# A decoder layer's first and last 40 microseconds, and the row stride of one operand

## The chip, the cores and the metric

The kernel runs on one core of a Trainium2 chip. The metric is the device time of one execution in microseconds. The kernel is one program, launched once, that computes the whole layer step in float32 (matrix products with operands split into two fp32r parts, see below).

## The reference, cut to what matters

One layer of a hybrid decoder is applied to 256 prompt tokens (one sequence) and to 64 sample tokens (8 sequences of 8, with past states). Both share all weights.

```python
D_MODEL = 2048; D_FF = 5504; LN_EPS = 1e-5; ALPHA = 2 ** 0.25

def layer(x, st, p):
    u = x @ w_in                                  # 2048 -> 6680
    q, k, v, o_pre, i_pre, f_pre, z, xbc, dt_pre = split_columns(u, SPLIT_SIZES)
    h_m, ... = mlstm_mixer(q, k, v, o_pre, i_pre, f_pre, ...)   # i_pre, f_pre: gates, 8 columns
    h_s, ... = ssd_mixer(z, xbc, dt_pre, ...)                   # dt_pre: 16 columns
    mix = concatenate([h_m, h_s]) @ w_out
    x = layer_norm(ALPHA * x + mix, ln1_g, ln1_b)
    f, fconv = conv_ffn(x, w_up, f_conv_w, f_conv_b, w_down, fconv0)   # 2048 -> 11008 -> 2048
    x = layer_norm(ALPHA * x + f, ln2_g, ln2_b)
    return x, new_states

def layer_norm(x, g, b):
    mu = mean(x); var = mean((x - mu) ** 2)
    return (x - mu) * rsqrt(var + LN_EPS) * g + b
```

## The kernel before, in words

All activations are kept transposed: 128 features on the partitions, 320 tokens (`NT` = 256 prompt + 64 sample) along the free dimension, 16 such blocks for the 2048 features. A product with a weight matrix is made of units of 128 output features. A unit is 16 blocks deep, and for each block there are three matmuls of 320 columns: high part of the weight by high part of the activation, high by low, low by high. Four blocks of a unit, 12 matmuls, are called a chunk here; `run_groups` works on two units in turn (four in the first group), chunk by chunk. For each chunk, `Stream.split_to` makes the high part on ScalarE (line 74) and the low part on VectorE (line 75), up to four chunks ahead of their use (`HB` = 5 buffers), from raw weights that SP's queue loads (line 61) into four buffers of 512 KB, plus four borrowed ones at the start.

Everything that is not such a product is written as background tasks, Python generators. The planner `Tasks` has a clock of its own: every matmul issued adds its estimated nanoseconds, and a task that yields a number sleeps for so many of them. After each chunk `run_groups` calls `tasks.pump`, which lets the tasks that are due issue their instructions. So the program order of every engine is fixed by hand and by this clock when the program is written; on the chip each engine works through its queue in that order.

The places that the change touches:

- The beginning. Nine fp32 matmuls of `ones` run on TensorE while the first loads arrive (`warm`). `x_load` brings x_prompt in four column chunks, `xs_load` brings x_sample into `xs_in`, whose lower 64 partitions hold the features below 1024 and the upper 64 those above. `x_transpose` turns a chunk's four blocks on TensorE (line 238), copies them to `XH` on ScalarE (line 416) and makes the remainder `XL` on VectorE (line 418). Block k < 8 also turns a piece of `xs_in`, which gives the sample columns of block k and of block k + 8. `start_x` and `each_x` place the first four blocks among the first chunk's matmuls, and the later ones ahead of the fourth unit's chunks.
- `keep_x`. For each of the four chunks of x it adds `XH` and `XL` on GpSimd, multiplies by the gate columns `gw` of `w_in` (matmuls with 32 output rows) and stores x to DRAM (`xT`) through SP. `gw` is loaded on SP behind the first eight raw weight tiles (lines 466 and 467), in pieces of 32 and 64 bytes. Ahead of its first chunk the task sleeps for 8000.
- The rows of the first norm. `dd` (the difference from the mean), and `DH` and `DL` (its high and low parts, with gain) are tiles of 16 rows of `NX` = 322 values: 320 tokens, and two further columns for the gain and the bias of the norm, which the first of three groups of up projections multiplies along (322 columns; the other two groups 320). The tile size is shared with the buffers `r01`, `r2`, `g` of the end.
- The end. `down_task` finishes a block of the output, turns it back to tokens on the partitions, takes `bn_stats` of it, and multiplies it by the norm's gain (`times_g`). After block 15, `bn_aggr` over 16 blocks' statistics, the reciprocal root (a square root on ScalarE and Newton steps on VectorE), three rows of factors, turned by TensorE into `nbr`, and a last loop over four column chunks: a matmul with the bias rows, a VectorE operation for the two prompt tiles (line 1676), and for the sample tile a ScalarE scale and copy and a GpSimd addition (lines 1671 to 1674). All stores go through SP.

Of the kernel before, what the change touches and what calls it, by code (L numbers as in the profile page):

```python
# [7 lines left out]
F32R = mybir.dt.float32r  # L8
# [5 lines left out]
NT = 320  # L14
# [156 lines left out]
def _hybrid_step(ctx, tc, I, O):  # L171
# [11 lines left out]
    def f32(ap):  # L183
        return ap.bitcast(F32)
# [199 lines left out]
    box = {}  # L384
    G.memset(ones, 1.0)
    warm = bank()
    for _ in range(9):
        mm(warm[:, 0:128], ones, ones, True, True)

    def x_load(c):  # L390
# [9 lines left out]
    def x_transpose(c, kks=range(4)):  # L400
        t = box["x", c]
        if kks[-1] == 3:
            flags.add(("xt", c))
            del box["x", c]
        for kk in kks:
            k = 4 * c + kk
            ps = bank()
            for i in range(2):
                transpose(ps[:, 128 * i:128 * i + 128], t[:, i, 128 * kk:128 * kk + 128])
            parts = [(k, 0, 256)]  # L410
            if k < 8:
                transpose(ps[:, 256:384], xs_in[:, 128 * k:128 * k + 128])
                parts = [(k, 0, NT), (k + 8, NT, 384)]
            parts = [(kx, slice(256 if a else 0, 256 if b == 256 else NT), ps[:, a:b]) for kx, a, b in parts]
            for kx, o, src in parts:
                A.activation(XH(kx)[:, o], src, AF.Copy)
            for kx, o, src in parts:
                V.tensor_tensor(XL(kx)[:, o], src, f32(XH(kx))[:, o], ALU.subtract)  # L418

    def keep_x():  # L420

        pg = bank()
        for c in range(4):
            yield from wait(("xt", c))
            yield 1000 if c else 8000
            ts = []
            for k in (4 * c, 4 * c + 2):
                t = mt("T4", [128, 2, NT])
                G.tensor_tensor(t, f32(XH(k, 2)), f32(XL(k, 2)), ALU.add)
                ts.append(t)  # L430
            yield 4000
            for kk in range(4):
                mm(pg[32 * kk:32 * kk + 32, 0:NT], gw[:, 4 * c + kk, :], ts[kk // 2][:, kk % 2, :], c == 0, c == 3)
            tasks.clk -= 3 * 541
            for k, t in zip((4 * c, 4 * c + 2), ts):
                dma(xT[:, k:k + 2, :], t)
        yield from gate_task(pg)


    xs_in = mt("T10", [128, 1024])  # L440
    xs_src = I["x_sample"].rearrange("b t f -> (b t) f")

    def xs_load(eng, a, b):
        for e in range(2):
            eng.dma_start(xs_in[64 * e:64 * e + 64, a:b], xs_src[:, 1024 * e + a:1024 * e + b])

    x_load(0)
    xs_load(nc.scalar, 0, 256)
    own = [mt("T4", [128, 1024]) for _ in range(4)]
    st.load(1, own[0:1])  # L450
    dma(box["x", 0][:, :, 256:512], I["x_prompt"][0, :, 256:512].rearrange("(i p) f -> p i f", p=128))
    xs_load(nc.sync, 256, 512)
    st.load(2, own[1:2])
    x_load(1)
    st.load(3, own[2:3])
    xs_load(nc.sync, 512, 1024)
    st.load(4, own[3:4])
    x_load(2)
    st.load(6)
# [846 lines left out]
    def start_x(u, s):  # L1306
        if u == s == 0:
            x_transpose(0, [0])
        if u == 3 and s < 3:
            x_transpose(s + 1)  # L1310

    def each_x(u, s, kk):
        if u == s == 0 and kk < 3:
            x_transpose(0, [kk + 1])


    MH, ML = Halves("MH"), Halves("ML")
# [33 lines left out]


    fp = ctx.enter_context(tc.tile_pool(name="fp", bufs=1))
    NX = NT + 2
    fr = tile_of(fp, {"big": (3, 16 * NX), "c": (12, 346), "rx": (2, 4 * NT), "rows": (2, 2304), "dg": (2, 384)})

    def fsm(shape, dt=F32):
        return fp.tile(shape, dt, name=nm("fsm"))
# [33 lines left out]
        rx[c] = t  # L1392

    load_rx(0)
    dd = fr("big", [128, 16, NX])
    DH, DL = fr("big", [128, 16, NX], F32R), fr("big", [128, 16, NX], F32R)
    s1, s2, kbc = fr("c", [128, NT]), fr("c", [128, NT]), fr("c", [128, NT])

    def out_task(m, ps):
# [153 lines left out]
    def down_task(j, m, ps):  # L1553
# [56 lines left out]
    for j in range(3):  # L1610
# [26 lines left out]

    mv, var, nb2, rs, u = fsm([128, 3, 2]), fsm([128, 3]), fsm([128, 3]), fsm([128, 3]), fsm([128, 3])  # L1640
    nbc, nbr = fsm([128, 3, 5], F32R), fr("dg", [5, 384], F32R)
    G.memset(f32(nbc), 1.0)
    for i in range(3):
        V.bn_aggr(mv[:, i, :], lnst[:, i, :, :])
    A.activation(fin["sd"], mv[:, :, 1], AF.Sqrt, bias=fin["eps"][:, 0:1])
# [7 lines left out]
    V.scalar_tensor_tensor(nb2, mv[:, :, 0], -1.0, rs, ALU.mult, ALU.mult)  # L1653
    V.tensor_copy(nbc[:, :, 0:2], bcl(nb2, 2))
    V.tensor_tensor(nbc[:, :, 2], nb2, f32(nbc[:, :, 0]), ALU.subtract)
    ps = bank()
    for i in range(3):
        transpose(ps[0:5, 128 * i:128 * i + 128], f32(nbc[:, i, :]))
    for i in range(3):
        t = slice(128 * i, 128 * i + 128)  # L1660
        V.tensor_copy(nbr[:, t], ps[0:5, t])
    times_g(15, fin["pt"])
    ys = O["y_sample"].rearrange("b t f -> (b t) f")
    for c in range(4):
        s = slice(512 * c, 512 * c + 512)
        for i in range(3):
            t = fin["r2"][:, s] if i == 2 else fin["r01"][:, i, s]
            w = bank()
            mm(w, nbr[:, 128 * i:128 * i + 128], fin["rows"][:, s], True, True)
            if i == 2:  # L1670
                A.activation(t, t, AF.Copy, scale=rs[64:128, i:i + 1])
                w2 = fr("rx", [128, 512])[64:128]
                A.activation(w2, w[64:128, :], AF.Copy)
                G.tensor_tensor(t, t, w2, ALU.add)  # L1674
            else:
                V.scalar_tensor_tensor(t, t, rs[:, i:i + 1], w, ALU.mult, ALU.add)
# [4 lines left out]
    dma(*late)  # L1681


# [62 lines left out]
```

## Time and profile before

| | |
|---|---|
| median of 3 runs | 1546.82 us (1544.77 to 1548.61) |
| the profiled execution | 1550.87 us, span of its instructions 1549.0 us |
| TensorE matmul / weight load busy | 98% / 96% of the span |
| VectorE, ScalarE, GpSimd busy | 63%, 50%, 20% |
| mean granted TensorE clock | 0.988 |
| moved by DMA | 254.39 MB, 164 GB/s over the span |

Times in the views are microseconds from the first instruction. A timeline row gives start, duration, engine, line, operation, what it writes and reads, the shape, how many instructions it merges, and in brackets how long the engine was idle before it and what ended that. A row of windows gives the window, its length, the busy time and the number of instructions of PE (TensorE matmuls), PEld (its weight loads), DVE (VectorE), ACT (ScalarE) and POOL (GpSimd), then the granted clock as a share of full speed, the DMA share and GB/s. An fp32 matmul appears as two records, so nine of them are 18.

### The profile page before, as it was taken

To read this page: it belongs to the slowest core of one execution; us is meant where nothing else is said; L and a number is where in the kernel's file an instruction comes from. 1 tells how busy PE (TensorE), PEld (TensorE's weight loads), DVE (VectorE), ACT (ScalarE), POOL (GpSimd) and SP (SyncE) were. 2 spreads that over 40 slices of the span, in tenths; PEclk is the share of its full clock that TensorE was granted. 3 is DMA by queue.
4 is the path that set the end of the run, shared out by engine and by line. 5 is a ranking of instruction groups with operands and counts; after the bars stand their busy time and mean duration, and the time that the engine had idled before them with its cause. 6 is when DMAs were issued, how large, how long until landed. Compare 5 with 4: busy or idle time off the path is not lost.

```text
span 1549.0 us, 28113 instructions
## 1 busy us (share of the span) xinstructions
PE 1521.4 (98%) x10518; PEld 1488.8 (96%) x10518; DVE 980.7 (63%) x1959; ACT 773.4 (50%) x1540; POOL 306.1 (20%) x651
## 2 busy tenths in 40 slices
PE   8999999999999999999999999999999999999996
PEld 7999999998999999999999999999999999999995
DVE  4676557666687587687777445566544555656765
ACT  3655434444545454566665345555433555555332
POOL 5213331134411142233330000000000000002201
PEclk8999999999999999999999999999999999999997
DMA  9556677577665554455544454554454555455542
GB/s 252 161 150 163 183 208 225 160 211 226 209 204 174 193 180 138 126 165 149 150 150 140 154 147 146 163 150 138 149 157 146 148 151 163 141 149 170 159 145 77
DMA packets 268900, 254.39 MB, mean 164 GB/s; under 512 B 18513, under 2 KB 263265, under 8 KB 268636
## 3 DMA queue, kind: packets, MB, share of 16 engines
q1 hardware_dynamic: 263612, 248.49, 53.8%
q0 software_dynamic: 4848, 3.91, 1.0%
q8 instruction: 82, 1.34, 0.4%
q14 instruction: 54, 0.44, 0.1%
q10 hardware_dynamic: 304, 0.20, 0.0%
HBM read 231.56 MB, written 20.43 MB: 163 GB/s over the span
## 4 chain that ended last, share of the span: by engine, by line
PE 93%; DVE 2%; DMA 2%; POOL 1%; ACT 1%; issue 1%; SPq 1%; POOLq 0%; DVEq 0%; ACTq 0%
PE bk L232 90%; PE bk L238 2%; DMA T<-w_in 1%; DVE lo L75 1%; DMA rx<-xT 0%; SPq L61 0%; ACT hi L74 0%; POOL big L1674 0%; SPq L466 0%; ACT MH L1320 0%; POOL T L193 0%; POOL T L968 0%; POOL T L811 0%; DVE HL L1531 0%; POOL T L981 0%
## 5 line engine op out<-in xcount | busy, mean ns | idle before, releaser
L75 DVE TENSOR_TENSOR lo<-raw,hi 128x512 fp32r<-128x512 f32 (+2 forms) x800 | 558.0, 708 | 393.5 <-ACT hi L74 390.6
L74 ACT ACTIVATE hi<-raw 128x512 fp32r<-128x512 f32 (+2 forms) x800 | 486.3, 616 | 454.3 <-PE bk L232 429.5
L232 PE MATMUL bk<-big,hi 128*128 128x320 f32 (+1 forms) x2752 | 609.5, 310 | 0.0
L232 PEld LDWEIGHTS bk<-big,hi 128*128 128x128 f32 x2752 | 462.1, 188 | 0.0
L232 PE MATMUL bk<-big,lo 128*128 128x320 f32 (+1 forms) x1376 | 426.6, 310 | 0.4 <-DVE lo L75 0.4
L232 PE MATMUL bk<-XH,hi 128*128 128x320 f32 x832 | 269.0, 323 | 0.8 <-ACT hi L74 0.8
L232 PEld LDWEIGHTS bk<-big,lo 128*128 128x128 f32 x1376 | 259.3, 188 | 0.7 <-DVE lo L75 0.7
L232 PE MATMUL bk<-XL,hi 128*128 128x320 f32 x832 | 258.9, 311 | 0.0
L232 PE MATMUL bk<-XH,lo 128*128 128x320 f32 x832 | 258.8, 311 | 0.0
L232 PE MATMUL bk<-HH,hi 128*128 128x320 f32 x688 | 214.2, 311 | 0.0
L232 PE MATMUL bk<-HH,lo 128*128 128x320 f32 x688 | 212.6, 309 | 0.0
L232 PE MATMUL bk<-HL,hi 128*128 128x320 f32 x688 | 212.5, 309 | 0.0
L232 PEld LDWEIGHTS bk<-XH,hi 128*128 128x128 f32 x832 | 158.1, 190 | 12.0 <-issue 7.9
L232 PEld LDWEIGHTS bk<-XL,hi 128*128 128x128 f32 x832 | 158.1, 190 | 0.9 <-DVE XL L418 0.4
L232 PEld LDWEIGHTS bk<-XH,lo 128*128 128x128 f32 x832 | 157.7, 190 | 0.2 <-DVE lo L75 0.2
L193 POOL TENSOR_SCALAR fst<-c 128x18 f32<-128x18 f32 x86 | 22.5, 269 | 566.9 <-ACT c L1508 566.7
L1515 DVE SCALAR_TENSOR_TENSOR c<-c,fcol,c 128x336 f32<-128x336 f32 x172 | 97.3, 567 | 58.4 <-ACT c L1513 55.3
L232 PEld LDWEIGHTS bk<-HL,hi 128*128 128x128 f32 x688 | 129.2, 188 | 0.0
L232 PEld LDWEIGHTS bk<-HH,hi 128*128 128x128 f32 x688 | 129.2, 188 | 0.0
L232 PEld LDWEIGHTS bk<-HH,lo 128*128 128x128 f32 x688 | 129.1, 188 | 0.0
L232 PE MATMUL bk<-MH,lo 128*128 128x320 f32 x256 | 80.1, 313 | 2.4 <-DVE lo L75 2.4
L232 PE MATMUL bk<-MH,hi 128*128 128x320 f32 x256 | 80.3, 314 | 0.3 <-ACT hi L74 0.3
(330 smaller groups left out, 1470.3 us busy)
## 6 DMA issues: line engine op xcount, KB each, us to landing
raw<-ffn_w_up SPq DMA_DIRECT2D x172, 512.0 KB, 3.9
raw<-w_in SPq DMA_DIRECT2D x100, 512.0 KB, 4.2
raw<-ffn_w_down SPq DMA_DIRECT2D x71, 512.0 KB, 3.5
raw<-w_out SPq DMA_DIRECT2D x32, 512.0 KB, 5.1
T<-state_mlstm_C SPq DMA_DIRECT2D x32, 256.0 KB, 5.5
s_C<-T SPq DMA_DIRECT2D x32, 256.0 KB, 4.0
T<-state_ssm SPq DMA_DIRECT2D x8, 512.0 KB, 6.9
s_ssm<-T SPq DMA_DIRECT2D x8, 512.0 KB, 6.7
```

Source lines behind the costliest of these rows:

```text
L74: nc.scalar.activation(h, src, AF.Copy)
L75: nc.vector.tensor_tensor(l, src, h.bitcast(F32), ALU.subtract)
L193: G.tensor_scalar(out, in_, 1.0, 0.0, ALU.mult, ALU.add)
L232: nc.tensor.matmul(out, lhsT=lhsT, rhs=rhs, start=start, stop=stop)
L238: nc.tensor.transpose(out, in_, ident[b:b + p, b:b + p])
L1515: V.scalar_tensor_tensor(c[:, 0:336], xp[:, j:j + 336], fcol[:, j, i:i + 1], c[:, 0:336], ALU.mult, ALU.add)
```

## The change

- Start: 13 warm matmuls instead of 9, and four more between the second block's transposes and the first real matmul. `xs_in` holds even blocks' features on the lower and odd blocks' on the upper partitions, so each even block's sample transpose gives the sample columns of itself and of the next block; x_sample's loads are cut into 512-byte runs, and the second of them stands behind one weight load instead of ahead of it. The first split of weights is issued ahead of the second block; blocks 3 and 4 of the first chunk are turned together ahead of the second block's matmuls. `keep_x` sleeps for 11500 instead of 8000.
- Rows: `dd`, `DH`, `DL` get rows of `NP` = 336 values (1344 bytes) instead of 322 (1288 bytes).
- End: the statistics of blocks 0 to 14 are aggregated after block 14 and put beside block 15's, so that the last aggregation reads three groups of three values for each tile of tokens; the reciprocal root is one power on GpSimd; six warm matmuls stand ahead of the last transposes; `times_g` of block 15 stands ahead of the copy to `nbr`, which is one copy instead of three; the last loop takes the sample tile first and stores it through ScalarE's queue.

```diff
-    for _ in range(9):
+    for _ in range(13):
         mm(warm[:, 0:128], ones, ones, True, True)
...
-            if k < 8:
-                transpose(ps[:, 256:384], xs_in[:, 128 * k:128 * k + 128])
-                parts = [(k, 0, NT), (k + 8, NT, 384)]
...
+            if k % 2 == 0:
+                transpose(ps[:, 256:384], xs_in[:, 64 * k:64 * k + 128])
+                parts = [(slice(0, NT), ps[:, 0:NT])]
+                box["xs"] = ps
+            else:
+                parts = [(slice(0, 256), ps[:, 0:256]), (slice(256, NT), box.pop("xs")[:, NT:384])]
...
-            yield 1000 if c else 8000
+            yield 1000 if c else 11500
...
-    xs_src = I["x_sample"].rearrange("b t f -> (b t) f")
+    xs_src = I["x_sample"].rearrange("b t (j e f) -> e (b t) j f", e=2, f=128)
...
-    xs_load(nc.sync, 256, 512)
     st.load(2, own[1:2])
+    xs_load(nc.sync, 2, 4)
...
         if u == s == 0:
             x_transpose(0, [0])
+            st.split_to(0)
+            x_transpose(0, [1])
+            for _ in range(4):
+                mm(warm[:, 0:128], ones, ones, True, True)
...
-        if u == s == 0 and kk < 3:
-            x_transpose(0, [kk + 1])
+        if u == s == 0 and kk == 1:
+            x_transpose(0, [2, 3])
...
-    NX = NT + 2
-    fr = tile_of(fp, {"big": (3, 16 * NX), ...
+    NX, NP = NT + 2, NT + 16
+    fr = tile_of(fp, {"big": (3, 16 * NP), ...
...
-    dd = fr("big", [128, 16, NX])
-    DH, DL = fr("big", [128, 16, NX], F32R), fr("big", [128, 16, NX], F32R)
+    dd = fr("big", [128, 16, NP])
+    DH, DL = fr("big", [128, 16, NP], F32R), fr("big", [128, 16, NP], F32R)
...
-            V.bn_stats(lnst[:, i, m, :], pt[:, 128 * i:128 * i + 128])
+            V.bn_stats(lnst[:, i, m, :] if m < 15 else agg[:, i, 3:9], pt[:, 128 * i:128 * i + 128])
         if m == 14:
-            A.activation(fin["sd"], fin["eps"], AF.Sqrt)
+            for i in range(3):
+                V.bn_aggr(amv[:, i, :], lnst[:, i, :, :])
+            V.tensor_copy(agg[:, :, 1], amv[:, :, 0])
+            V.tensor_scalar(agg[:, :, 2], amv[:, :, 1], 1920.0, 2048.0 * LN_EPS, ALU.mult, ALU.add)
...
     for i in range(3):
-        V.bn_aggr(mv[:, i, :], lnst[:, i, :, :])
-    A.activation(fin["sd"], mv[:, :, 1], AF.Sqrt, bias=fin["eps"][:, 0:1])
-    V.tensor_scalar(var, mv[:, :, 1], LN_EPS, None, ALU.add)
-    V.reciprocal(rs, fin["sd"])
-    V.tensor_tensor(u, rs, rs, ALU.mult)
-    V.tensor_tensor(u, u, var, ALU.mult)
-    V.tensor_scalar(var, u, 0.375, -1.25, ALU.mult, ALU.add)
-    V.tensor_tensor(u, u, var, ALU.mult)
-    V.scalar_tensor_tensor(rs, u, 1.875, rs, ALU.add, ALU.mult)
+        V.bn_aggr(mv[:, i, :], agg[:, i, :])
+    G.tensor_tensor(rs, mv[:, :, 1], nhalf, ALU.pow)
...
+    warm = bank()
+    for _ in range(6):
+        mm(warm[:, 0:256], ones, fin["g"][:, 0:256], True, True)
...
-    for i in range(3):
-        t = slice(128 * i, 128 * i + 128)
-        V.tensor_copy(nbr[:, t], ps[0:5, t])
     times_g(15, fin["pt"])
+    V.tensor_copy(nbr, ps[0:5, 0:384])
...
-        for i in range(3):
+        for i in (2, 0, 1):
...
                 G.tensor_tensor(t, t, w2, ALU.add)
+                if c:
+                    nc.scalar.dma_start(*late)
+                late = ys[:, s], t
...
-        if c:
-            dma(*late)
-        late = ys[:, s], fin["r2"][:, s]
-    dma(*late)
+    nc.scalar.dma_start(*late)
```

More of the change, by code (lines that the diff above doesn't have):

```diff
@@ L409, in x_transpose @@
                 transpose(ps[:, 128 * i:128 * i + 128], t[:, i, 128 * kk:128 * kk + 128])
-            parts = [(k, 0, 256)]
-            if k < 8:
-                transpose(ps[:, 256:384], xs_in[:, 128 * k:128 * k + 128])
-                parts = [(k, 0, NT), (k + 8, NT, 384)]
[L414 to L418, printed above, removed]
+            if k % 2 == 0:
[4 more added lines that the diff above has]
+                parts = [(slice(0, 256), ps[:, 0:256]), (slice(256, NT), box.pop("xs")[:, NT:384])]
+            for o, src in parts:
+                A.activation(XH(k)[:, o], src, AF.Copy)
+            for o, src in parts:
+                V.tensor_tensor(XL(k)[:, o], src, f32(XH(k))[:, o], ALU.subtract)
     def keep_x():
@@ L440, in _hybrid_step @@
     xs_in = mt("T10", [128, 1024])
-    xs_src = I["x_sample"].rearrange("b t f -> (b t) f")
+    xs_src = I["x_sample"].rearrange("b t (j e f) -> e (b t) j f", e=2, f=128)
     def xs_load(eng, a, b):
         for e in range(2):
-            eng.dma_start(xs_in[64 * e:64 * e + 64, a:b], xs_src[:, 1024 * e + a:1024 * e + b])
+            eng.dma_start(xs_in[64 * e:64 * e + 64, 128 * a:128 * b].rearrange("p (j f) -> p j f", f=128), xs_src[e][:, a:b, :])
     x_load(0)
-    xs_load(nc.scalar, 0, 256)
+    xs_load(nc.scalar, 0, 2)
     own = [mt("T4", [128, 1024]) for _ in range(4)]
@@ L451, in _hybrid_step @@
     dma(box["x", 0][:, :, 256:512], I["x_prompt"][0, :, 256:512].rearrange("(i p) f -> p i f", p=128))
-    xs_load(nc.sync, 256, 512)
     st.load(2, own[1:2])
+    xs_load(nc.sync, 2, 4)
     x_load(1)
     st.load(3, own[2:3])
-    xs_load(nc.sync, 512, 1024)
+    xs_load(nc.sync, 4, 8)
     st.load(4, own[3:4])
@@ L1353, in _hybrid_step @@
     fp = ctx.enter_context(tc.tile_pool(name="fp", bufs=1))
-    NX = NT + 2
-    fr = tile_of(fp, {"big": (3, 16 * NX), "c": (12, 346), "rx": (2, 4 * NT), "rows": (2, 2304), "dg": (2, 384)})
+    NX, NP = NT + 2, NT + 16
+    fr = tile_of(fp, {"big": (3, 16 * NP), "c": (12, 346), "rx": (2, 4 * NT), "rows": (2, 2304), "dg": (2, 384)})
     def fsm(shape, dt=F32):
@@ L1535, in _hybrid_step @@
     fin = {}
-    lnst = fsm([128, 3, 16, 6])
+    lnst, agg, amv = fsm([128, 3, 15, 6]), fsm([128, 3, 9]), fsm([128, 3, 2])
     def fstate():
@@ L1627, in _hybrid_step @@
             gdma(fin["g"], I["ln2_g"].broadcast_to([128, D]))
-            fin["eps"], fin["sd"] = fsm([128, 3]), fsm([128, 3])
-            G.memset(fin["eps"], LN_EPS)
+            G.memset(agg[:, :, 0], 1920.0)
             tasks.add(gb_rows())
@@ L1636, in _hybrid_step @@
     tasks.drain()
-    mv, var, nb2, rs, u = fsm([128, 3, 2]), fsm([128, 3]), fsm([128, 3]), fsm([128, 3]), fsm([128, 3])
+    mv, nb2, rs, nhalf = fsm([128, 3, 2]), fsm([128, 3]), fsm([128, 3]), fsm([128, 3])
     nbc, nbr = fsm([128, 3, 5], F32R), fr("dg", [5, 384], F32R)
+    G.memset(nhalf, -0.5)
     G.memset(f32(nbc), 1.0)
     for i in range(3):
-        V.bn_aggr(mv[:, i, :], lnst[:, i, :, :])
-    A.activation(fin["sd"], mv[:, :, 1], AF.Sqrt, bias=fin["eps"][:, 0:1])
-    V.tensor_scalar(var, mv[:, :, 1], LN_EPS, None, ALU.add)
-    V.reciprocal(rs, fin["sd"])
-    V.tensor_tensor(u, rs, rs, ALU.mult)
-    V.tensor_tensor(u, u, var, ALU.mult)
-    V.tensor_scalar(var, u, 0.375, -1.25, ALU.mult, ALU.add)
-    V.tensor_tensor(u, u, var, ALU.mult)
-    V.scalar_tensor_tensor(rs, u, 1.875, rs, ALU.add, ALU.mult)
+        V.bn_aggr(mv[:, i, :], agg[:, i, :])
+    G.tensor_tensor(rs, mv[:, :, 1], nhalf, ALU.pow)
     V.scalar_tensor_tensor(nb2, mv[:, :, 0], -1.0, rs, ALU.mult, ALU.mult)
```

## The prediction

> **What bounds the kernel now.** I read the page first: engine shares, the granted clock, the chain that ended last.
>
> ```profile
> span 1549.0 us, 28113 instructions
> PE 1521.4 (98%) x10518; PEld 1488.8 (96%) x10518; DVE 980.7 (63%) x1959; ACT 773.4 (50%) x1540; POOL 306.1 (20%) x651
> PEclk8999999999999999999999999999999999999997
> PE 93%; DVE 2%; DMA 2%; POOL 1%; ACT 1%; issue 1%; SPq 1%; POOLq 0%; DVEq 0%; ACTq 0%
> ```
>
> TensorE is busy 98% of the span and holds 93% of the chain; the clock is short only in the first and the last slice. So there are three things to win: the two ends, and the pace of a matmul between them. The change touches all three. Next the chain of the first 60 us, and the windows and the timeline around its DMA piece.
>
> ```profile
> 21.88 10.25 DMA T<-w_in
> 32.27 8.92 PE bk L232 x44
> 28.00:32.00 4.00, 0.97 (x7) 0.70 (x5) 1.76 (x4) 0.95 (x2) 0.00 (x0) 0.94 0.57 62
> 32.00:36.00 4.00, 3.73 (x17) 2.74 (x18) 0.00 (x0) 0.00 (x0) 0.00 (x0) 0.50 0.98 290
> 36.00:40.00 4.00, 4.00 (x21) 4.00 (x21) 0.71 (x2) 1.26 (x2) 0.00 (x0) 0.71 0.43 133
> 28.66 0.31 PE L232 MATMUL bk<-XH,lo 128*128 128x320 f32 x1
> 32.27 1.30 PE L232 MATMUL bk<-T,T 128*32 128x320 f32 x8 [3.30 <-DMA T<-w_in]
> 33.92 0.47 PE L232 MATMUL bk<-XL,hi 128*128 128x320 f32 x1
> 34.19 0.47 PE L232 MATMUL bk<-XH,lo 128*128 128x320 f32 x1
> 38.97 0.31 PE L232 MATMUL bk<-XL,hi 128*128 128x320 f32 x1
> 39.12 0.31 PE L232 MATMUL bk<-XH,lo 128*128 128x320 f32 x1
> 44.47 0.75 PE L232 MATMUL bk<-T,T 128*32 128x320 f32 x8
> ```
>
> At 28.97 us TensorE reaches the gate matmuls of `keep_x`; their weights `gw` (the L467 load) land at 32.13. It idles 3.30 us, and the granted clock falls to 0.50: matmuls start 0.27 us apart (33.92, 34.19) and are back at 0.15 (38.97, 39.12) only after 38.3.
>
> **Part 1, the later gate matmuls.** `keep_x` resumes by the planner's clock, not by time. A chunk of 12 matmuls adds 12 x 136 = 1628 ns, a transpose 108, an fp32 matmul of 128 columns 216. Today: first pump at 2924, +8000 = 10924, reached after the sixth chunk (12361); +4000, so the gate matmuls follow the eighth (16481), as the rows show. After: first pump at 3574 (10 transposes and 4 warm matmuls ahead of it), +11500 = 15074, reached after the eighth chunk (17131); +4000 = 21131, so they follow the eleventh (22016). That is 36 matmuls or 36 x 0.147 = 5.3 us later: 28.97 - 0.5 (part 2) + 5.3 = 33.8 us, against 32.13. The weights' place in SP's queue stays; x_sample's packets become 512 bytes, and 1.6 us of margin covers a later landing. The wait goes (-3.30). With it goes the half clock: 18 matmuls between 33.57 (32.27 + 1.30) and 38.3 at 0.27 instead of 0.147 us (the pace of part 3; 2.2) and the gate group's 1.30 against 0.75 us (0.55). Together **-6.0 us**. Bounds: -3.3, if the clock halves anyway, and -6.3. Nothing becomes late in its place: the weight splits run four chunks ahead, and raw tiles 8 and 9, queued on SP behind that load, are first used by the 17th chunk, which in program order stands well behind the row at 44.47. `keep_x`'s xT stores on SP move behind later raw loads, which helps those. What comes later by 5 us is the gate chain. The mixer's tasks hang on it, and in the page's slices TensorE shows no gap under them; costed at nothing, ±1.5, three waits of the size of the one at 42.34 (0.50, below).
>
> The Trainium skill's page "TensorE: Matmul & The Clock Gate", Part 1, says that the clock falls to half after at least one idle window of 3413 ns, at a free-running phase. By that rule 3.30 us of idling need not halve anything and the term would be -3.3; the trace differs, with 0.50 granted right behind 3.30 us.
>
> **Part 2, the start.**
>
> ```profile
> 1.00 3.78 PE L232 MATMUL bk<-ones 128*128 128x128 f32 x18 [1.00 <-POOL ones L385]
> 7.30 0.84 PE L238 MATMUL bk<-ident,T 128*128 128x128 f32 x4 [2.31 <-DMA T<-x_sample]
> 8.90 0.63 PE L232 MATMUL bk<-XH,hi 128*128 128x320 f32 x1 [0.76 <-ACT hi L74]
> 11.50 0.84 PE L238 MATMUL bk<-ident,T 128*128 128x128 f32 x3
> 12.38 0.55 ACT L416 ACTIVATE XH<-bk 128x320 fp32r<-128x320 f32 x2 [0.89 <-PE bk L238]
> 12.81 2.71 ACT L74 ACTIVATE hi<-T 128x512 fp32r<-128x512 f32 x5
> 14.21 0.41 PE L232 MATMUL bk<-XH,hi 128*128 128x320 f32 x1
> 42.34 0.44 PE L238 MATMUL bk<-ident,T 128*128 128x128 f32 x2 [0.50 <-DVE XL L418]
> ```
>
> The second chunk starts at 14.21: behind the fourth block's transposes, its ACT copies (12.38), and its own weights' split, on ACT from 12.81 and then on DVE, 1.4 us. The four more warm matmuls at the front lie inside the 2.31 us wait. The other four (3.78/9 = 0.42 us each, half clock) run from 8.14 to 9.8 and hold the first real matmul 0.9 us back from 8.90. In return transposes 3 and 4 come together behind the first three matmuls: about 9.8 + 0.8 + 1.3 = 11.9, copies till 12.4, split till 13.8, so -0.4; **-0.5 us**, with a little for the clock that the warm work keeps up. Ends: +0.9, nothing regained; -1.8, full clock throughout. The x_sample load that moves behind a weight load is not needed before the fourth chunk's transposes. One new cost: an even block's PSUM bank is now held until the odd block has copied its sample half. At 42.34, where three banks are free for four transposes and today's wait is 0.50 us for one eviction, one more pair of small copies comes first: **+0.4 us** (0 to 0.8).
>
> **Part 3, the row stride.** dd, DH and DL rows go from 1288 to 1344 bytes. Pace of pure matmul stretches, two of each count being in flight at the window's start (HH; then DH/DL with 320 and with 322 columns):
>
> ```profile
> 820.60:919.10 98.50, 98.50 (x674) 98.50 (x673) 51.96 (x97) 42.54 (x80) 0.00 (x0) 1.00 0.50 156
> 919.16:1116.50 197.34, 197.34 (x1346) 197.34 (x1345) 117.59 (x210) 111.11 (x238) 17.27 (x84) 1.00 0.50 147
> 663.79:802.90 139.11, 139.11 (x936) 139.11 (x936) 107.03 (x222) 87.79 (x181) 46.95 (x91) 1.00 0.52 153
> ```
>
> 98.50/672 = 146.6 ns with HH's rows of 1280 bytes; 197.34/1344 = 146.8 and 139.11/934 = 148.9 with the 1288-byte rows. If the new rows run like HH's: 2784 x 0.25 = 0.7, and 1344 x (148.9 - 146.6 x 322/320 = 1.4) = 1.9, together -2.6. The other end is +1.2, if a constant offset costs as much again as 322 columns lose now. I take **-1.5**, nearer the HH rows, not all of it: in the program as built HH starts at byte 54848 of a partition, a multiple of 64, but the three tiles at 119136, 139744 and 160352, each 32 past one, and the change moves nothing ahead of them. Every row would then start 32 past a multiple. DVE, ACT and POOL work on these rows is of unchanged size and covered.
>
> **Part 4, the end.**
>
> ```profile
> 1529.48 0.55 DVE L1557 TENSOR_TENSOR big<-big,bk 128x128 f32<-128x128 f32 x2 [1.75 <-PE bk L232]
> 1531.18 1.47 DVE L1644 BATCH_NORM_AGGREGATE fsm<-fsm 128x2 f32<-128x96 f32 x3
> L1259 DVE BATCH_NORM_AGGREGATE sm<-sm x12: 181/182/184, 381.6 to 486.1; 128x2 f32<-128x6 f32 x12
> 1532.74 0.30 ACT L1645 ACTIVATE fsm<-fsm,fsm 128x3 f32<-128x3 f32 x1 [9.61 <-DVE fsm L1644]
> 1534.27 0.16 DVE L1653 SCALAR_TENSOR_TENSOR fsm<-fsm,fsm 128x3 f32<-128x3 f32 x1
> 1534.73 0.17 DVE L1655 TENSOR_TENSOR fsm<-fsm,fsm 128x3 fp32r<-128x3 f32 x1
> 1535.88 0.68 DVE L1661 CAST dg<-bk 5x128 fp32r<-5x128 f32 x3 [0.98 <-PE bk L238]
> 1537.23 5.36 DVE L1676 SCALAR_TENSOR_TENSOR big<-big,fsm,bk 128x512 f32<-128x512 f32 x8
> 1537.90 0.59 ACT L1673 ACTIVATE rx<-bk 64x512 f32<-64x512 f32 x1 [2.92 <-PE bk L232]
> 1538.39 0.70 ACT L1671 ACTIVATE big<-big,fsm 64x512 f32<-64x512 f32 x1
> 1538.63 5.10 POOL L1674 TENSOR_TENSOR big<-big,rx 64x512 f32<-64x512 f32 x4 [91.45 <-DVE big L1676]
> 1544.69 0.55 SPq L1681 DMA_DIRECT2D y_sample<-big  x1
> L193 POOL TENSOR_SCALAR fst<-c 128x18 f32<-128x18 f32 x86 | 22.5, 269 | 566.9 <-ACT c L1508 566.7
> ```
>
> Three aggregates of 9 instead of 96 values: 3 x 0.18 for 1.47, -0.9. Square root and Newton steps, 1532.65 to 1534.27, become one POOL power: no row shows one; between 0.27 (the small POOL row) and 1.27 (a quarter of the 5.10), I take 0.4 + 0.1 of hand-over, near the small row: -1.1. From 1534.90 to the ACT copy at 1537.90 is 3.0; now `times_g` (0.67, from the casts' end at 1536.56 to 1537.23) covers the transposes, and one cast (0.55, between a third of the 0.68 and all of it) and one matmul (0.5) follow: 1.8, -1.2. The six warm matmuls lie in that wait. Then a loss: the sample stores move to ACT's queue. ACT's round of copy and scale, 0.59 + 0.70, already matches POOL's 1.27; a store's issue of 0.55 in the later rounds makes it 1.8, so the last POOL addition ends 7.4 instead of 5.8 us behind the first copy. Against it the last store no longer queues on SP behind the prompt's (1.0 us between POOL's end, 1543.73, and 1544.69): +0.7 net. The early aggregates after block 14 (3 x 0.53 + 2 x 0.17 = 1.9) don't quite fit DVE's 1.75 us gap: +0.2. Sum **-2.3** (-0.6 to -3.4).
>
> **Sum.** -6.0 - 0.5 + 0.4 - 1.5 - 2.3 = -9.9 us on the profiled execution (1550.87, span 1549.0): 1541. That execution is 4.05 above the median of the runs. Where the clock windows fall differs by run, so I count half of the 2.75 us of half clock for the median: -8.6, **1538.2 us**.
>
> **Rivals.**
> - The wait moves. `keep_x` or what follows it meets a late input elsewhere, or the gate chain's delay reopens idling ahead of the out projection. Only parts 2 to 4 are won, 3.9 us: 1542.9. Against it stands the 1.6 us margin. 0.11.
> - The alignment does nothing (rows 32 past a line, or pace set by columns alone): 1539.7. 0.25. The skill's clock page ("Wait — 56ns, not 53.3ns?") has a matmul at columns/2.4 GHz + 2.5 ns whatever its addresses, 135.8 ns for 320; the trace disagrees on the pace (146.6), and on two strides sharing one.
> - The other side: every row now straddles lines alike. If that cost one 16-element step (6.7 ns at full clock) per matmul, 4128 of them lose 27 us: 1565. It outweighs the rest from 2.1 ns on. Today's straddling rows run at 146.8 with 320 columns, which speaks against it. 0.04.
> - The forecast as summed: 0.60, own range 1534 to 1541.5.
>
> A difference under 0.3% (4.6 us) is about what a measurement can't tell from none. Faster by more: 0.60 + 0.25 + a little of the first rival = 0.86; same 0.10; slower 0.04. The range, 1533 to 1543, takes in the forecast, the void alignment and, at its edge, the moved wait.
>
> **What would show it.** The timeline at 28 to 38 us without idling and at full clock; gate matmuls behind the eleventh chunk; second chunk near 13.7; pace of DH/DL stretches at 146.6 and 147.5; 322-column pace unchanged if the alignment is void; POOL's power under 0.5 us; ACT's rounds of 1.8 us at the end. A gate load landing after 34 us, or an idle above 1 us in the mixer, would make it wrong.

## The result, and the profile after

The changed kernel takes 1539.85 us in the median (1538.19 to 1541.05), the kernel before beside it 1547.71 (1544.77 to 1548.94): a ratio of 0.9945 with a 95% interval of 0.9931 to 0.996, or 7.9 us less: a difference that is clear of the noise, though small. The profiled execution takes 1540.23 us against 1550.87, 10.6 us less.

The page of the changed kernel:

```profile
span 1538.5 us, 28146 instructions
PE 1517.5 (99%) x10546; PEld 1485.2 (97%) x10546; DVE 983.9 (64%) x1955; ACT 771.4 (50%) x1537; POOL 312.0 (20%) x653
PEclk9999999999999999999999999999999999999998
PE 93%; DVE 3%; DMA 1%; ACT 1%; issue 1%; POOL 0%; POOLq 0%; ACTq 0%; SPq 0%; DVEq 0%
```

TensorE holds the same share of the chain; what changed is the first and the last digit of the clock (8 to 9, 7 to 8) and DMA's share of the chain (2% to 1%, while VectorE's goes from 2% to 3%). Next the windows of the changed kernel's first 36 us (columns as before: PE, PEld, DVE, ACT, POOL, granted clock, DMA share, GB/s), then its TensorE timeline.

```profile
4.00:8.00 4.00, 3.05 (x26) 2.84 (x26) 0.33 (x1) 0.78 (x2) 3.02 (x7) 1.00 1.05 312
8.00:12.00 4.00, 3.65 (x22) 2.75 (x20) 2.71 (x8) 2.55 (x8) 3.33 (x7) 1.00 1.10 312
28.00:32.00 4.00, 4.00 (x27) 3.71 (x26) 3.02 (x7) 2.72 (x7) 0.00 (x0) 1.00 0.68 100
32.00:36.00 4.00, 3.16 (x27) 2.21 (x26) 1.67 (x4) 1.34 (x5) 0.00 (x0) 1.00 0.98 277
```

```profile
7.22 1.06 PE L232 MATMUL bk<-ones 128*128 128x128 f32 x8
...
11.79 0.31 PE L232 MATMUL bk<-XH,hi 128*128 128x320 f32 x1
...
27.66 0.41 PE L232 MATMUL bk<-XL,hi 128*128 128x320 f32 x1 [0.67 <-DVE XL L419]
...
33.29 0.75 PE L232 MATMUL bk<-T,T 128*32 128x320 f32 x8
...
35.90 0.44 PE L238 MATMUL bk<-ident,T 128*128 128x128 f32 x2 [0.84 <-DVE XL L419]
```

The clock is full in every one of these windows. The second chunk begins at 11.79 instead of 14.21; the gate matmuls stand at 33.29 without a bracket, so TensorE doesn't idle ahead of them, and they take 0.75 instead of 1.30 us. Two waits for `XL` are there instead: 0.67 at 27.66, which is new, and 0.84 at 35.90, which was 0.50. The lead has to be read where both kernels have done the same work. At chunk 22 (55.88 instead of 63.18) they have not: the kernel before is then done with all four groups of gate matmuls, the changed one with three. At the 27th chunk both are done with them and with the task that follows; its first matmul, before and after:

```profile
73.45 0.31 PE L232 MATMUL bk<-XH,hi 128*128 128x320 f32 x1
```

```profile
66.95 0.31 PE L232 MATMUL bk<-XH,hi 128*128 128x320 f32 x1
```

The lead is 6.50 us, and it stays 6.50 to the 57th chunk.

In the changed kernel's long stretches of pure products (HH; DH/DL with 320 columns; with 322), two matmuls are again in flight at the window's start:

```profile
813.00:911.40 98.40, 98.40 (x673) 98.40 (x672) 51.64 (x97) 42.43 (x80) 0.00 (x0) 1.00 0.51 156
911.55:1108.40 196.85, 196.85 (x1345) 196.85 (x1344) 117.45 (x210) 110.89 (x238) 17.29 (x84) 1.00 0.50 148
665.00:802.00 137.00, 137.00 (x926) 137.00 (x925) 105.16 (x216) 85.13 (x174) 44.80 (x86) 1.00 0.51 151
```

HH: 98.40/671 = 146.6 ns a matmul, as before. DH/DL with 320 columns: 196.85/1343 = 146.6 instead of 146.8; with 322 columns 137.00/924 = 148.3 instead of 148.9 in this window (148.4 instead of 148.8 from start to start over the whole 322-column stretch).

The end, in the changed kernel's timeline, from the last subtraction:

```profile
1520.97 0.55 DVE L1563 TENSOR_TENSOR big<-big,bk 128x128 f32<-128x128 f32 x2 [0.18 <-PE bk L232]
...
1522.66 0.31 DVE L1654 BATCH_NORM_AGGREGATE fsm<-fsm 128x2 f32<-128x9 f32 x3
1523.13 0.89 POOL L1655 TENSOR_TENSOR fsm<-fsm,fsm 128x3 f32<-128x3 f32 x1 [84.42 <-DVE fsm L1654]
...
1524.45 0.17 DVE L1658 TENSOR_TENSOR fsm<-fsm,fsm 128x3 fp32r<-128x3 f32 x1
...
1526.44 0.59 ACT L1677 ACTIVATE rx<-bk 64x512 f32<-64x512 f32 x1 [1.67 <-PE bk L232]
...
1527.45 6.24 SPq L1684 DMA_DIRECT2D y_prompt<-big  x8
...
1530.38 2.50 POOL L1678 TENSOR_TENSOR big<-big,rx 64x512 f32<-64x512 f32 x2 [0.71 <-ACT rx L1677]
```

And the same place of the kernel before, one row that was not shown:

```profile
1538.00 2.31 SPq L1677 DMA_DIRECT2D y_prompt<-big  x4
```

From the start of the last product matmul (1529.13 before, 1520.62 after) to the end of the span it was 19.86 us and is 17.83: -2.0. The piece from the first prompt store to the end has not changed, 10.99 before (1538.00 to 1548.99) and 11.01 after (1527.45 to 1538.46).

Cut at the same matmuls, the two profiled executions differ by this (us; the first matmul of 322 columns starts at 605.34 before and 597.89 after):

| stretch | before | after | difference |
|---|---|---|---|
| start of the span to the 27th chunk | 73.45 | 66.95 | -6.50 |
| to the first matmul of 322 columns | 531.89 | 530.94 | -0.95 |
| to the last product matmul | 923.79 | 922.73 | -1.06 |
| to the end of the span | 19.86 | 17.83 | -2.03 |

### The profile page after: what moved, and what is told of

Read it like the earlier page. It is cut to its first block, busy times and chain, and to the rows that moved or that the text cites. A ratio compares the mean times of both kernels' runs of the same rounds, so it can differ in the third digit from the quotient of the medians.

```text
span 1538.5 us, 28146 instructions
## 1 busy us (share of the span) xinstructions
PE 1517.5 (99%) x10546; PEld 1485.2 (97%) x10546; DVE 983.9 (64%) x1955; ACT 771.4 (50%) x1537; POOL 312.0 (20%) x653
## 4 chain that ended last, share of the span: by engine, by line
PE 93%; DVE 3%; DMA 1%; ACT 1%; issue 1%; POOL 0%; POOLq 0%; ACTq 0%; SPq 0%; DVEq 0%
PE bk L232 91%; PE bk L238 2%; DVE lo L75 1%; DMA T<-d_m 0%; DMA T<-x_sample 0%; DMA raw<-w_in 0%; POOL big L1678 0%; ACT hi L74 0%; DVE big L1421 0%; DVE big L1425 0%; DVE XL L419 0%; DVE HL L1537 0%; DVE big L1408 0%; DVE rx L1613 0%; DVE big L1438 0%
```

## Experiments

Each kernel's diff is against the kernel before where its label begins with g, and against the changed kernel where it begins with a. Single executions of one kernel differ by up to 6 us, as much as most parts of this change are worth, so parts are read from the traces, and medians only where they carry it.

**The sleep alone** (g_gate).

```diff
-            yield 1000 if c else 8000
+            yield 1000 if c else 11500
```

> The kernel before with keep_x's sleep of 11500 alone. By the planner's clock the gate matmuls then follow the eleventh chunk, where TensorE arrives at about 28.97 + 5.28 = 34.25 us; the load lands near 32.1. Theory A (the wait and the half clock behind it are the main gain): no idle before the gate matmuls, full clock from 14.4 us on, the 21st chunk starts 6.0 us earlier than before (57.2 instead of 63.2), the median falls by 4.5 to 6. Theory B (the wait moves elsewhere, the load is what holds the start): an idle of 1 us or more before the gate matmuls or soon behind them, the 21st chunk less than 3 us earlier.

Measured: median 1542.71 against 1547.12, ratio 0.9971 (0.9961 to 0.9982), -4.4 us. Its timeline:

```profile
13.52 0.31 PE L232 MATMUL bk<-XH,hi 128*128 128x320 f32 x1
...
33.52 0.74 PE L232 MATMUL bk<-T,T 128*32 128x320 f32 x8
...
35.56 0.44 PE L238 MATMUL bk<-ident,T 128*128 128x128 f32 x2 [0.50 <-DVE XL L418]
```

The gate matmuls wait for nothing at 33.52, and the stall behind them keeps its 0.50. The 27th chunk starts at 66.62: 6.8 us ahead of the kernel before, and 5.2 and 5.4 ahead of two other traces with the old start and the old sleep (71.84 in g_rows, 71.97 in g_end). Those have one stretch of half clock at the gate, 3.4 us long, where the execution shown of before has two. More than half of the whole gain is this one number.

**The start without the sleep** (g_start): the hunks of the start as in the change, `keep_x` left at 8000.

```diff
-    for _ in range(9):
+    for _ in range(13):
...
             yield 1000 if c else 8000
```

> The kernel before with the new start (warm matmuls, layout and order of x_sample, order of the first transposes), keep_x's sleep left at 8000. The second chunk starts near 11.8 us instead of 14.2, as in the changed kernel. Theory A (the gate load's landing at 32.1 us is a fixed point): TensorE comes to the gate matmuls 2 us earlier and waits 2 us longer, about 5.3 us, so the 21st chunk starts within 0.6 us of before and the median does not move (within 1.5 us). Theory B (the start's gain stands by itself): idle before the gate matmuls stays at 3.3 us and the 21st chunk starts 2 us or more earlier.

Measured: 1548.3 against 1547.12, ratio 1.0009 (1.0001 to 1.0018): no gain, rather a loss. The timeline of this kernel, at the gate matmuls:

```profile
31.74 1.30 PE L232 MATMUL bk<-T,T 128*32 128x320 f32 x8 [4.30 <-DMA T<-w_in]
```

The second chunk starts at 12.11, earlier than in any trace of the old start (13.52 to 14.21), but the gate matmuls, held by the load of their columns, start at 31.74, nearly when they did (32.27; 31.83 in g_rows), so the wait is 4.30 instead of 3.30 us (5.3 was expected). The 27th chunk starts at 72.22, against 71.84 and 71.97 in g_rows and g_end: whatever the start gains ahead of this wait is lost in it. Why the median is even 1.2 us higher the trace doesn't show.

**The start with the sleep** (g_gatestart): both edits above.

> The kernel before with the new start and the sleep of 11500 together; rows and end as before. Alone the start moved the median by +1.2 us (ratio 1.0009) and the sleep by -4.4 (0.9971). Theory A (the start's gain is only swallowed by the wait for the gate load, and shows once the gate matmuls stand later): about -6.5 us, ratio 0.9955 to 0.9962, clearly below the sleep alone; no idle over 0.3 us before the gate matmuls. Theory B (the start brings nothing): the sleep's own ratio, 0.996 to 0.998.

Measured: 1542.93 against 1547.87, ratio 0.9965 (0.9952 to 0.9977), -4.9 us, not to be told from the sleep alone (0.9961 to 0.9982). Its timeline:

```profile
11.91 0.30 PE L232 MATMUL bk<-XH,hi 128*128 128x320 f32 x1
...
27.39 0.42 PE L232 MATMUL bk<-XL,hi 128*128 128x320 f32 x1 [0.28 <-DVE XL L419]
...
33.02 0.75 PE L232 MATMUL bk<-T,T 128*32 128x320 f32 x8
...
35.63 0.44 PE L238 MATMUL bk<-ident,T 128*128 128x128 f32 x2 [0.84 <-DVE XL L419]
```

This trace and that of g_gate differ by the start alone. The second chunk is 1.61 us ahead (11.91 against 13.52), the gate matmuls 0.50 (33.02 against 33.52), and at the last transposes of x the lead is gone (35.63 against 35.56). In the third chunk of x, an even block now turns a piece of x_sample too, so there are 10 transpose records and 6 `XL` copies where the old order has 8 and 4. VectorE, here and in g_gate:

```profile
26.86 2.10 DVE L419 TENSOR_TENSOR XL<-bk,XH 128x320 fp32r<-128x320 f32 x6
```

```profile
26.98 1.40 DVE L418 TENSOR_TENSOR XL<-bk,XH 128x256 fp32r<-128x256 f32 x4
```

TensorE comes to this chunk's first `XL` 1.3 us earlier (its ninth chunk starts at 26.81 instead of 28.14), the copies start only 0.12 earlier, and there are six of them: the ninth chunk takes 2.61 instead of 1.76 us. At the fourth chunk of x the wait grows from 0.50 to 0.84. The 27th chunk starts at 66.69, in g_gate at 66.62.

**The changed kernel without the four later warm matmuls, and with the old nine** (a_nowarm).

```diff
-    for _ in range(13):
+    for _ in range(9):
...
-            for _ in range(4):
-                mm(warm[:, 0:128], ones, ones, True, True)
```

> The changed kernel with nine warm matmuls at the start as before, and none between the second block's transposes and the first real matmul. The prediction's step had the four later ones hold the first matmul back by 0.9 us at half clock and give back little. Theory A (they keep the clock granted): the clock falls to half for one or two windows of 3.4 us near 8 us, the second chunk starts 1 to 2.4 us later than the changed kernel's 11.8, median 1 to 2 us higher. Theory B (they only cost time): second chunk no later, at most 12.0.

Measured: 1539.87, ratio 0.9946 (0.9934 to 0.9959), the changed kernel's own. Windows of this kernel:

```profile
5.35:8.76 3.41, 0.73 (x5) 0.31 (x3) 0.49 (x1) 1.10 (x3) 2.06 (x5) 1.00 1.08 317
8.76:12.18 3.42, 3.40 (x13) 3.15 (x14) 2.04 (x6) 1.53 (x6) 2.36 (x5) 0.50 1.09 319
```

And of the changed kernel, whose clock is full from 4.24 on:

```profile
4.24:7.65 3.41, 2.46 (x22) 2.25 (x22) 0.00 (x0) 0.44 (x1) 2.55 (x5) 1.00 1.05 311
```

With 0.73 us of TensorE work in the 3.41 us up to 8.76 the clock halves, for 3.42 us; the changed kernel has 2.46 in such a stretch and keeps it. (The Trainium skill, "TensorE: Matmul & The Clock Gate", Part 1, gives 3413 ns as the clock gate's window; this trace agrees.) In all nine traces with the longer warm work the clock stays full here, and in all five without it falls between 7.6 and 9 us. So the warm work does what it is for: the second chunk starts at 11.79 (11.8 to 12.6 in the nine) instead of 12.86. But half of that 1.1 us is gone by the 27th chunk, and its 67.47 lies among those of the kernels with the changed start and sleep (66.69 to 68.01); the median shows nothing of it either.

**The rows alone** (g_rows).

```diff
-    NX = NT + 2
+    NX, NP = NT + 2, NT + 16
...
-    DH, DL = fr("big", [128, 16, NX], F32R), fr("big", [128, 16, NX], F32R)
+    DH, DL = fr("big", [128, 16, NP], F32R), fr("big", [128, 16, NP], F32R)
```

> The kernel before with the row stride of 1344 bytes alone; the rows still begin 32 bytes past a multiple of 64. Theory A (a stride that is a multiple of 64 makes the pace constant, wherever the rows begin): 146.67 ns for each matmul of 320 columns of DH and DL instead of 146.87 on average, 148.3 instead of 148.8 with 322 columns, together 1.2 us, not to be seen in the median (within 2 us). Theory B (the paces of the changed kernel come from its other edits): paces unchanged from before, changing from matmul to matmul.

Measured: 1547.36, ratio 0.9998 (0.999 to 1.0007), nothing that the median can tell. Windows of the two DH/DL stretches, 320 and 322 columns:

```profile
914.80:1111.70 196.90, 196.90 (x1345) 196.90 (x1344) 117.41 (x210) 110.92 (x238) 17.31 (x84) 1.00 0.50 148
665.00:802.00 137.00, 137.00 (x925) 137.00 (x925) 104.94 (x215) 86.24 (x178) 47.56 (x91) 1.00 0.52 153
```

196.90/1343 = 146.6 ns and 137.00/923 = 148.4, as in the changed kernel. Single gaps from start to start vary in both kernels, from 141 to 152 ns with 320 columns before, from 142 to 150 here; but with the new rows every chunk of 12 has the same mean, 146.67 and 148.33, while with the 1288-byte rows it changes from chunk to chunk (145.6 to 147.9, and 147.4 to 150.1). From the first matmul of 322 columns to the last product matmul it is 922.8 us, and 923.7 to 923.8 in the five traces with the old rows: 1.0 us, in every trace.

**Rows that do begin at multiples of 64** (a_base64). In the changed kernel as built, the three tiles are at bytes 119136, 140640 and 162144 of a partition, 32 past a multiple of 64, and with a stride of 1344 so is every row. Here a small tile ahead of them is 32 bytes larger, and they stand at 119168, 140672 and 162176.

```diff
-    fcol = fp.tile([128, 4, 86], ...)
+    fcol = fp.tile([128, 352], F32, name="fcol")[:, 0:344].rearrange("p (a b) -> p a b", b=86)
```

> The changed kernel with a spacer of 32 bytes ahead of the three tiles, so that every row of dd, DH and DL really begins at a multiple of 64 bytes. Theory A (only the stride counts): pace as in the changed kernel, 146.67 ns with 320 columns and 148.33 with 322. Theory B (the place where a row begins counts too): 322 columns at 147.5 ns, the pace of two more columns, 1.1 us less over that phase, 320 columns unchanged.

Measured, in one execution: 1537.68. Its windows of the two stretches:

```profile
910.08:1106.20 196.12, 196.12 (x1344) 196.12 (x1343) 117.44 (x210) 110.41 (x238) 17.36 (x84) 1.00 0.50 148
665.00:802.00 137.00, 137.00 (x924) 137.00 (x923) 104.55 (x218) 84.73 (x174) 44.82 (x85) 1.00 0.51 149
```

196.12/1342 = 146.1 and 137.00/922 = 148.6: faster than in the changed kernel with 320 columns, slower with 322 (chunks of 147.4 and 149.8 in turn). Neither account has either pace. From the first matmul of 322 columns to the last product matmul it is 921.5 us, 1.3 less than in the changed kernel.

**Two more strides**: 1296 bytes with the tiles as in the change (a_np324), and 1408, a multiple of 128, with the small tile enlarged (a_np352).

```diff
-    NX, NP = NT + 2, NT + 16
+    NX, NP = NT + 2, NT + 4
```

> The changed kernel with rows of 324 values, 1296 bytes, a multiple of 16 bytes but not of 64. Theory A (64 bytes is the unit): the pace changes from matmul to matmul again, about 146.9 ns on average with 320 columns. Theory B (16 bytes are enough): constant 146.67 ns.

```diff
-    NX, NP = NT + 2, NT + 16
+    NX, NP = NT + 2, NT + 32
```

> The changed kernel with tiles at a multiple of 64 bytes, as in the run with the spacer, and a row stride of 1408 bytes, a multiple of 128 as the 1280 of HH's rows is (1344 is not). Theory A (rows that alternate between the halves of 128 bytes are what gave 146.11 ns with 320 columns): 146.67 ns as HH's. Theory B (the tiles' places or something else make it): 146.11 again or another pace.

Measured: 1539.78 and 1538.88, one execution each. Windows of the 320-column stretch with 1296 bytes, then of both stretches with 1408:

```profile
910.84:1107.40 196.56, 196.56 (x1344) 196.56 (x1344) 117.42 (x210) 110.59 (x238) 17.32 (x84) 1.00 0.50 148
```

```profile
911.61:1107.70 196.09, 196.09 (x1344) 196.09 (x1343) 117.42 (x210) 110.61 (x238) 17.42 (x84) 1.00 0.50 148
665.00:802.00 137.00, 137.00 (x915) 137.00 (x914) 103.75 (x214) 83.96 (x172) 43.29 (x83) 1.00 0.51 149
```

196.56/1342 = 146.5 (and 148.3 with 322 columns); 196.09/1342 = 146.1, and 137.00/913 = 150.1. At 320 columns DH and DL run at 146.1 with their rows at multiples of 64, with either stride, at 146.6 with rows 32 past, and at 146.5 and 146.8 with mixed starts; at 322 the multiples of 128 are the slowest of all. But HH's rows, 1280 bytes apart from byte 54848 on, are at multiples of 64 too and run at 146.6. So neither multiples of 64 nor halves of 128 bytes explain the pace, and what sets it stays open.

**The end alone** (g_end): the hunks of the end as in the change.

```diff
+    G.tensor_tensor(rs, mv[:, :, 1], nhalf, ALU.pow)
...
-        for i in range(3):
+        for i in (2, 0, 1):
```

> The kernel before with the new end alone. From the last product matmul's start to the span's end 17.9 us as in the changed kernel, instead of 19.9; power on GpSimd 0.9 us; the median 1 to 2.5 us lower. Theory A (the stores' traffic sets the end): from the first prompt store's issue to the last packet 9.4 us, as before. Theory B (ScalarE, held up by issuing stores, sets the end): the last packet belongs to a sample store and comes more than 3 us behind its issue on ScalarE's queue, with no prompt store landing behind it.

Measured: 1546.38, ratio 0.9993 (0.9984 to 1.0002). In its trace the tail from the last product matmul is 18.09 us (19.86 before, 17.83 with the whole change), and the first prompt store stands 11.26 us ahead of the end. The saving of 1.8 us is there; the median can't tell it from none.

**Sample stores back on SP** (a_spstore), each behind the next column chunk's, as before the change.

```diff
-                if c:
-                    nc.scalar.dma_start(*late)
-                late = ys[:, s], t
...
+        if c:
+            dma(*late)
+        late = ys[:, s], fin["r2"][:, s]
...
-    nc.scalar.dma_start(*late)
+    dma(*late)
```

> The changed kernel with the sample stores back on SP's queue, behind the prompt's, as before the change. The step of the prediction (a store's issue of 0.55 us on ScalarE lengthens each round and the last addition by 1.6 us): GpSimd's four additions run without the 0.7 us pause and end 5.8 instead of 6.4 us behind the first copy. Theory A (the stores' traffic sets the end): the program ends within 0.4 us of the changed kernel all the same, counted from the first store's issue. Theory B (ScalarE sets it): it ends 0.6 us or more earlier.

Measured: 1539.52, ratio 0.9952 (0.9939 to 0.9966), like the changed kernel. Its timeline, and a window behind its last issue:

```profile
1525.72 4.96 POOL L1678 TENSOR_TENSOR big<-big,rx 64x512 f32<-64x512 f32 x4 [3.16 <-ACT rx L1677]
1525.99 2.31 SPq L1681 DMA_DIRECT2D y_prompt<-big  x4
...
1532.67 0.59 SPq L1685 DMA_DIRECT2D y_sample<-big  x1
```

```profile
1531.00:1533.00 2.00, 0.00 (x0) 0.00 (x0) 0.00 (x0) 0.00 (x0) 0.00 (x0) 0.50 0.98 283
```

GpSimd's four additions run without a pause and end 0.75 us earlier behind the first copy than in the changed kernel (5.69 against 6.44), but from the first prompt store to the end it is 10.85 against 11.01 us. Work that ends 0.75 us sooner brings 0.16.

**Three of the eight prompt stores not written** (a_halfstore).

```diff
-                dma(O["y_prompt"][0, 128 * i:128 * i + 128, s], t)
+                if i == 0 or c == 0:
+                    dma(O["y_prompt"][0, 128 * i:128 * i + 128, s], t)
```

> The changed kernel without three of the eight prompt stores at the end (0.79 MB of 2.62 MB are not written). Theory A (the stores' traffic sets the end): at the 320 GB/s of that stretch the span from the first prompt store's issue to the end of the program shrinks by 2.4 us, from 11.05 to about 8.7, until ScalarE's and GpSimd's chain is the longer one, about 9.5. Theory B (ScalarE's issues and GpSimd's additions set the end): unchanged within 0.4 us.

Measured, in one execution: 1537.84. GpSimd's chain keeps its 6.43 us, and the first store to the end shrinks from 11.01 to 9.79. A window behind the additions, here, then two windows of the changed kernel, then two of the kernel before:

```profile
1532.30:1534.30 2.00, 0.00 (x0) 0.00 (x0) 0.00 (x0) 0.00 (x0) 0.00 (x0) 0.50 0.50 152
```

```profile
1532.45:1534.45 2.00, 0.00 (x0) 0.00 (x0) 0.00 (x0) 0.00 (x0) 0.43 (x1) 0.50 1.00 331
1534.45:1536.45 2.00, 0.00 (x0) 0.00 (x0) 0.00 (x0) 0.00 (x0) 0.00 (x0) 0.50 0.97 312
```

```profile
1542.00:1544.00 2.00, 0.00 (x0) 0.00 (x0) 0.58 (x1) 0.39 (x1) 1.72 (x2) 0.50 0.99 319
1544.00:1546.00 2.00, 0.00 (x0) 0.00 (x0) 0.00 (x0) 0.00 (x0) 0.00 (x0) 0.50 0.99 317
```

In both kernels all 16 DMA engines are full at 312 to 331 GB/s until about 2 us from the end, 3 us and more after GpSimd is done. 2.62 MB of outputs at some 320 GB/s are 8.2 of the 11.0 us: the stores' traffic, not who issues them or when the last addition ends, sets the end. Take 0.79 MB of it away and the end comes 1.2 us sooner; the last packets are then those of the sample store on ScalarE's queue.

**What the runs point to** (a_best): the changed kernel with the tiles of a_base64, the sample half of the fourth chunk's even blocks copied early, the last loop in the order 0, 2, 1, and the sample stores but the last on SP.

```diff
-        for i in (2, 0, 1):
+        for i in (0, 2, 1):
```

> The changed kernel with three more edits: the spacer of 32 bytes (320 columns at 146.1 ns, 322 at 148.7, together -1.1 us); for the last chunk of x the sample half of an even block's bank is copied at once, so that the bank is free for the fourth block's transposes (the idle of 0.84 us at 35 us back to 0.5, -0.3); a prompt tile first in the last loop and the sample stores but the last on SP's queue (first store 0.25 us earlier, -0.25). Theory: 1.6 us below the changed kernel, ratio to the kernel before about 0.9935, hardly to be told from the changed kernel's 0.9945 by the median, but in the profile by the stages. Rival: SP's queue, waiting for a sample tile, holds the prompt stores and the end grows by 0.5 us or more.

Measured: 1538.09, ratio 0.9934 (0.992 to 0.9947), beside 0.9946 of a_nowarm on the same chip: 1.8 us less in the median, inside the intervals. The early copy does nothing (the stall stays 0.84), and the tail stays (17.89 against 17.83): the first prompt store comes 0.25 us sooner after the last product matmul, the end no sooner. The row pace is all that its trace shows as gain: 921.5 instead of 922.7 us for the stretch of the table that holds these rows, as in a_base64.

## Why the prediction was right, point by point

It said 1538.2 for the median (1533 to 1543), and -9.9 us on the profiled execution; measured are 1539.85 and -10.6. (Its terms give 1538.3: half of 2.75 off -9.9 is -8.5, not -8.6.) The large term was right for its reason. The closeness of the sum owes something to luck: the table above has -6.5 where parts 1 and 2 have -6.1, -1.1 for part 3's -1.5, -2.0 for part 4's -2.3, and -0.95 between them, in the mixer, where the prediction had nothing, give or take 1.5. That last piece isn't shown to come from the change: it takes 529.3 to 531.9 us in the four traces with the old sleep and 528.1 to 530.9 in the ten with the new one. That the median lies next to 1539.7, the rival without any effect of the rows, is chance too, as the rows did gain 1.0 us.

- **Part 1, -6.0 on the profiled execution, -4.6 on the median** (half of the 2.75 us of half clock left out): right, in mechanism and size. The sleep alone brings -4.4 in the median (-6.0 to -2.8). The gate matmuls stand at 33.29 (33.8 predicted), no idle and no half clock. The step of halving the clock's share for the median is borne out: the execution shown of before has two stretches of half clock at the gate (31.5 to 38.3), g_rows, g_end and g_start have one (32.8 to 36.2 in g_rows), and g_rows and g_end are 1.6 and 1.5 us ahead of it at the 27th chunk.
- **Part 2, -0.5 and +0.4**: the sum of -0.1 is right, its steps are not, and that is luck. The first term was too small: the second chunk comes at 11.79, not 13.8 or 13.7, -2.4 instead of -0.5. Of these 2.4, 1.1 are the clock that the warm matmuls keep full (a_nowarm), and 0.7 belong to the execution shown of before, with two stretches of half clock at the start where g_gate and g_rows have one (13.52 and 13.56); the rest is the new order. The step that failed is the hold-back: the four later warm matmuls were costed at 4 x 0.42 at half clock, but ran at full clock (1.06 us for all), and the first real matmul came at 8.35, ahead of the 8.90 of before. What took the gain back is one cost put right and one that the prediction had at nothing. The stall is +0.34 where +0.4 was expected. The other is VectorE at the third chunk of x, with a new 0.67 us wait at 27.66, as the chain of the changed kernel shows at that place (start, duration, what):

```profile
24.61 2.60 DVE lo L75 x2
27.20 0.41 DVE XL L419
27.61 0.04 issue
27.66 6.38 PE bk L232 x43
```

TensorE comes here 1.5 us earlier than in g_gate, and VectorE no earlier (first `XL` copy at 27.13, against 26.98), with six copies to make instead of four; the ninth chunk takes 3.00 us instead of 1.76. The weight splits ahead of the copies take 1.4 to 2.0 us each while GpSimd's `keep_x` additions run (18.96 to 26.05) and 0.68 after them. That the additions are what slows them is likely, but no run shows it.
- **Part 3, -1.5**: mis-sized by 0.4, right in kind. The 320-column pace came as put (146.6), the 322-column one at 148.3 to 148.4 instead of 147.5, so that term is 0.5 (1344 x 0.4) where equal pace per column would give 1.9. The note that every row as built begins 32 past a multiple of 64 mattered: with true multiples DH and DL run at 146.1. That the alignment does nothing, and that rows all 32 past a multiple lose a step on every matmul (1565), are both excluded by the traces. No run shows that 64 bytes is a unit for these reads, as the word "line" in the rivals supposes. The Trainium skill, "TensorE: Matmul & The Clock Gate", "Wait — 56ns, not 53.3ns?", gives columns divided by 2.4 GHz plus about 2.5 ns from start to start, which for 320 columns is an estimate of 135.8 ns. That section doesn't speak of addresses; the traces differ, with 146.1 to 146.9, by where the rows lie.
- **Part 4, -2.3**: measured -2.0, and the pieces tell why; the traces with the new end as in the change have tails of 17.8 to 18.4 us, those with the old end 19.7 to 19.9, so -2.0 is near the upper end of what it brings. From the last product matmul to the last small VectorE row: -1.8 predicted (aggregates -0.9, power -1.1, early aggregates +0.2), 5.77 to 4.00 measured, -1.77. That this agrees is luck, as no piece of it came as put: the power took 0.89, not 0.4 (its bounds were 0.27 and 1.27: nearest to the small row was the wrong end), the aggregates 0.31 instead of 0.54, and the early aggregates cost nothing, with 0.18 us of idle left ahead of the last subtraction. The ACT copy came 1.82 instead of 3.0 us behind, -1.2 as predicted, but that term was measured at the wrong instruction: the loop now begins with the sample tile, and the first prompt store came only 0.27 sooner (2.83 us behind that row's end, at 1524.62, against 3.10). The step "+0.7 from ACT's issue" is wrong as a cause: the last addition ends 6.44, not 7.4, behind the first copy, and a_spstore removes the pause for 0.16 us. (The Trainium skill, "DMA: Bandwidth & Descriptors", Issuing engines are not separate DMA queues, says that the engines that issue share the same 16 DMA engines, and only issue time is saved; a DMA share of 0.97 to 1.00 with ScalarE's issues and of 0.98 with SP's agrees.) -1.77 - 0.27 + 0.02 = -2.0.

The rival of the moved wait had something: waits did move to 27.66 and 35.90, for 1.5 us together where 0.5 was before, not for the whole of part 1. What stays open: the parts measured alone add up to less in their medians (-4.9 for sleep and start, -0.7 and +0.2 for end and rows, -5.4 together) than the whole (-7.9). Their intervals (sleep and start -7.4 to -3.6, end -2.5 to +0.3, rows -1.5 to +1.1) leave room for it, and for the 1.8 and 1.0 that the traces show for end and rows.

## What to carry to other kernels

Before putting a task earlier or later by a planner's clock, find when its slowest input lands: here one number, moved past a DMA's landing, was worth more than all the rewriting of both ends, and speed ahead of such a wait was worth nothing (4.30 us of idling for 3.30). At the end of a kernel look at the DMA share first: where it stays at 1.00, who issues the stores was worth 0.16 us and less traffic 1.2, and a term must be counted to the first store. Even that is no promise: in a_best it came 0.25 us earlier and the end did not. A stage's gain is real only at the last place where the old order still waits, and where both orders have done the same background work; compare the two traces there, not where the edit is.

## What the runs showed of the hardware that was not expected

- The pace of a 320-column matmul at full clock changes with where its moving rows lie: for DH and DL 146.1 ns at multiples of 64 bytes, 146.6 at 32 past them, 146.8 with changing starts; with 322 columns 148.3 to 150.1, and the best place for one is not the best for the other. HH at multiples of 64 runs at 146.6, so there is more to it than the start of a row.
- From the first matmul of 322 columns to the last product matmul, executions of the same rows agree within 0.1 us (923.7 to 923.8, 922.7 to 922.8), so a change of 1 us can be read there that the medians can't tell.
- A power of 128x3 values on GpSimd takes 0.89 us, three times that engine's 0.27 us small operation; an aggregate of 9 values 0.1 us on VectorE when three follow one another.
- The clock fell without TensorE being idle for a whole stretch of 3.4 us: 0.73 us of work in 3.41 (a_nowarm, up to 8.76 us) and 0.90 (the kernel before, 28.07 to 31.48) were too little, 2.46 (the changed kernel) and 2.13 (g_start, up to 7.67 us) enough. Where the border lies isn't shown: in the mixer 1.91 was enough once (a_spstore, up to 417.12 us), and 2.13 was not (the kernel before, up to 417.19).
